# Seven block products for one gate and up projection, and a grouped down projection, in a two-layer backbone block

## The chip, the cores and the metric

The kernel runs on one core of a Trainium2 chip. The metric is the device time of one execution in microseconds (us). Engines are named as the profile names them: PE is TensorE (its matrix products; PEld are its weight loads), DVE is VectorE, ACT is ScalarE, POOL is GpSimd, and SP issues the transfers.

## What is computed

A block of two layers works on 512 latent tokens of 1024 features (plus 256 context tokens in layer 0). Each layer is a mixer and a SwiGLU feed-forward network (FFN) with 2816 hidden features, both behind a modulated RMS norm and a gated residual:

```
mod = silu(c) @ ada_w[i] + ada_b[i]
sh1, sc1, g1, sh2, sc2, g2 = split(mod, 6)
hx = rms_norm(x, norm_mix[i]) * (1 + sc1) + sh1
x = x + g1 * mixer_i(hx)              # layer 0: attention and SSD; layer 1: gated short convolution
h = rms_norm(x, norm_ffn[i]) * (1 + sc2) + sh2
x = x + g2 * ((silu(h @ w_gate) * (h @ w_up)) @ w_down)
...
return rms_norm(x, final_norm)
```

## The kernel before

Activations are kept transposed, features on the 128 partitions and tokens along the columns: xT is 8 tiles (k) of 128 x 512. The 512 tokens are often handled as two halves (e = 0, 1) of 256. A matrix is multiplied in float32r with a split: value = hi + lo, and `mm3` issues three products for each 128 x 128 block, hi x hi, hi x lo and lo x hi.

Weights come in the order of one list, `plan`. `weight` loads 128 x 1024 values into a staging tile (wst, 3 buffers), ScalarE casts them to whi (L94) and VectorE subtracts to get wlo (L95); both have 3 buffers. `take` hands out the next piece and asks for the one two places further. At two seams a fourth buffer from another pool (`extra`) is used, so that three pieces for the next stage and the one behind them can be ready.

After a mixer or an FFN, `project` multiplies by the output weights, adds into xT (L916) and squares for the next norm. Its last tiles (`tail`: 3 after the mixers, 1 after the FFNs) are done in halves of 256 columns, first half 0 of all, then half 1. For each half a job `renorm` is put in the list `due`: after 3500 further columns of products it issues the statistics (L333) and nine tiny VectorE instructions for the inverse root (L142 to L150), after 8500 more the broadcast (L307), and then `entry`, which makes the modulated activation of that half, k by k, and splits it into act_hi and act_lo (L945 to L952). `mm3` counts the columns by `tick`; `flush` issues what is left, and `tick` with a huge count goes on through the whole list.

In `ffn` the first three pieces are multiplied together by `together` (the joint loop), k outermost, first half 0 and then half 1, so that TensorE can follow the entry. Then come 22 hidden tiles f, each gate and up with 24 products of 512 columns, into PSUM (psS); `finish` applies silu and the product and splits into ffn_h. All 22 hidden tiles are kept; only then `project` runs over them with 66 products for each of 8 output tiles. During FFN 0 the generator `ada_rest` computes modulation rows in the background: each step is one load of 256 KB (ada_st) and one VectorE instruction (L257), a product with the constant `fold` ends it, and `pump(3)` lets it advance three steps after each piece.

TensorE's instructions are issued in the order in which the program writes them. The other engines' queues are ordered by a scheduler at build time, by that order and by its own expectation of when operands are ready; on the chip every queue runs in order.

Of the kernel before, what the change touches and what calls it, by code (L numbers as in the profile page):

```python
# [7 lines left out]
F32 = mybir.dt.float32  # L8
# [31 lines left out]
NCON = CAT[-1]  # L40

# [12 lines left out]

def halves(ap):
    return ap.rearrange("p (a b) -> p a b", a=2)


class Block:
    def __init__(self, ctx, tc, t):  # L60
# [3 lines left out]
        self.plan, self.ready, self.used = [], [], 0  # L64
# [6 lines left out]
        self.plan += [(t["w_o"][d], 1024) for d in range(KC)]  # L71
        for i in range(2):
            if i == 1:
                self.plan += [(t["w_sc"][j, x], 1024, j == 0 and x == 1) for j in range(KC) for x in (1, 2, 0)]
                self.plan += [(t["w_so"][d], 1024) for d in range(KC)]
            self.plan += [(t["w_gu"][i, f, x], 1024, f + x == 0) for f in range(NF) for x in range(2)]
            for d in range(KC):
                self.plan += [(t["w_dn"][i, d, :, k:min(k + KC, NF), :], P * min(KC, NF - k)) for k in range(0, NF, KC)]
# [17 lines left out]

    def take(self, ahead=2):
        n = self.used
        self.used += 1
        for i in range(len(self.ready), min(n + ahead + 1, len(self.plan))):  # L100
            self.ready.append(self.weight(*self.plan[i]))
        w, self.ready[n] = self.ready[n], None
        return w

    def weight(self, src, n, extra=False):
# [3 lines left out]
        hi, lo = ((self.np if extra else self.wp).tile([P, 1024], F32R, name=x, tag=x, bufs=1 if extra else 3)  # L109
                  for x in ("whi", "wlo"))  # L110
        self.split(hi[:, :n], lo[:, :n], st[:, :n])
        return hi, lo
# [123 lines left out]
    def ada_rest(self, pool, layer, parts, acc=None, bufs=2, tag=None):  # L236
# [3 lines left out]
        for n, part in enumerate(parts):  # L240
            for j in range(2):
# [4 lines left out]
                for k in range(0, KC, step):  # L246
                    if acc is None:
# [91 lines left out]
    def hybrid(self):  # L339
# [5 lines left out]
        with tc.tile_pool(name="start", bufs=1) as sp:  # L345
# [22 lines left out]
            def weights():  # L368
                for i in range(3):
                    self.ready.append(self.weight(*self.plan[i]))  # L370
# [526 lines left out]
    def project(self, xt, m, gate, between, nk=KC, order=None, tail=1, lead=0, more=True):  # L897
# [32 lines left out]
        ws = [load(2 + more - i) for i in range(tail)]  # L930
# [6 lines left out]
    def entry(self, xt, i, j):  # L937
        nc = self.nc
        gsc, sh = self.gsc[:, i, j, :], self.mod[:, i, 3 * j, :]

        def run(e, rb):
            ts = slice(TC * e, TC * e + TC)
            for k in range(KC):
                u = self.np.tile([P, TC], F32, name="nm_u", tag="nm_u", bufs=3)
                nc.vector.tensor_tensor(u, xt[:, k, ts], rb, ALU.mult)  # L945
                if k % 2:
                    nc.vector.tensor_scalar(u, u, gsc[:, k:k + 1], sh[:, k:k + 1], ALU.mult, ALU.add)
                else:
# [193 lines left out]
```

## Time and profile before

| | |
|---|---|
| median of 3 runs | 1294.58 us (1290.67 to 1295.09) |
| the profiled execution | 1294.68 us, span 1292.9 us |
| mean granted TensorE clock | 0.989 of full speed |
| busy: PE, DVE, ACT, POOL | 1241.5, 731.7, 448.0, 182.7 us |
| FFN 0 | about 370 to 735 us |
| short convolution layer | about 735 to 916 us |
| FFN 1 | about 916 to 1281 us |

The span is from the first to the last instruction of the profiled execution; the time has 1.8 us around it. Products are pipelined, and a product's own duration is longer than the distance to the next one: for TensorE the starts are to be read. The granted clock 1.00 is 2.4 GHz, and 0.50 is 1.2 GHz.

### The profile page before, as it was taken

How to read it: one execution, taken by the hardware profiler on the slowest of the kernel's cores; microseconds unless marked ns; L12 is line 12 of the kernel's file. 1: busy time of each engine (PE TensorE's matmuls, PEld its weight loads, DVE VectorE, ACT ScalarE, POOL GpSimd, SP SyncE). 2: the span in 40 equal slices, each digit the busy share in tenths (PEclk: the TensorE clock that was granted, in tenths of full speed). 3: DMA queues.
4: the chain of work that ended last, by engine and by line, in shares of the span. 5: the costliest groups of instructions: out<-in, count | busy, mean ns of one | idle time of the engine just before them, and what ended most of it. 6: DMA issues, size and time to landing. Idle time of an engine off the chain costs nothing.

```text
span 1292.9 us, 15877 instructions
## 1 busy us (share of the span) xinstructions
PE 1241.5 (96%) x6086; PEld 1022.4 (79%) x6086; DVE 731.7 (57%) x1187; ACT 448.0 (35%) x675; POOL 182.7 (14%) x199
## 2 busy tenths in 40 slices
PE   5999988899999999999999999999999999999997
PEld 3887665567798888888888988888988888888886
DVE  4898899976464777788522564443643333332223
ACT  4534534455353222222222342223532222222221
POOL 3433435440220000000000110002200000000001
PEclk9998989999999999999999999999999999999998
DMA  9331453300413777777433323333133333333322
GB/s 370 125 98 49 123 166 119 98 1 1 149 63 122 229 250 241 226 235 255 123 102 90 115 67 97 98 98 114 50 114 98 98 98 98 92 96 90 92 88 66
DMA packets 54845, 158.52 MB, mean 123 GB/s; under 512 B 6000, under 2 KB 8688, under 8 KB 54512
## 3 DMA queue, kind: packets, MB, share of 16 engines
q1 hardware_dynamic: 54480, 157.20, 38.3%
q8 instruction: 48, 0.79, 0.3%
q10 hardware_dynamic: 288, 0.31, 0.1%
q14 instruction: 29, 0.24, 0.1%
HBM read 154.86 MB, written 2.10 MB: 121 GB/s over the span
## 4 chain that ended last, share of the span: by engine, by line
PE 83%; DVE 9%; issue 3%; DMA 3%; POOL 1%; ACT 1%; SPq 0%; DVEq 0%; ACTq 0%; POOLq 0%
PE psS L116 14%; PE psS L117 14%; PE psS L118 14%; PE psA L116 10%; PE psA L118 10%; PE psA L117 10%; PE psV L830 2%; DMA adaw<-ada 2%; PE psS L961 1%; DVE xtok L257 1%; DVE mx L804 1%; PE psS L822 1%; DVE wlo L95 1%; PE psS L963 1%; DMA xT<-xT 1%
## 5 line engine op out<-in xcount | busy, mean ns | idle before, releaser
L95 DVE TENSOR_TENSOR wlo<-wst,whi 128x1024 fp32r<-128x1024 f32 (+2 forms) x194 | 234.9, 1214 | 317.2 <-ACT whi L94 311.8
L94 ACT CAST whi<-wst 128x1024 fp32r<-128x1024 f32 (+2 forms) x194 | 198.4, 1026 | 549.9 <-PE psS L117 258.5
L116 PE MATMUL psS<-act_hi,whi 128*128 128x512 f32 x760 | 297.5, 391 | 1.0 <-DVE cs_a L573 0.9
L118 PE MATMUL psS<-act_hi,wlo 128*128 128x512 f32 x760 | 297.2, 391 | 0.0
L117 PE MATMUL psS<-act_lo,whi 128*128 128x512 f32 x760 | 297.2, 391 | 0.0
L118 PEld LDWEIGHTS psS<-act_hi,wlo 128*128 128x128 f32 x760 | 143.3, 189 | 30.0
L116 PEld LDWEIGHTS psS<-act_hi,whi 128*128 128x128 f32 x760 | 143.2, 188 | 29.3 <-issue 1.2
L117 PEld LDWEIGHTS psS<-act_lo,whi 128*128 128x128 f32 x760 | 143.2, 188 | 27.7
L325 POOL TENSOR_TENSOR sq_acc<-sq_acc,sq 128x512 f32<-128x512 f32 (+1 forms) x28 | 38.0, 1356 | 872.2 <-issue 645.7
L116 PE MATMUL psA<-ffn_h_hi,whi 128*128 128x512 f32 (+1 forms) x396 | 145.4, 367 | 0.0
L117 PE MATMUL psA<-ffn_h_lo,whi 128*128 128x512 f32 (+1 forms) x396 | 145.0, 366 | 0.0
L118 PE MATMUL psA<-ffn_h_hi,wlo 128*128 128x512 f32 (+1 forms) x396 | 145.0, 366 | 0.0
L257 DVE SCALAR_TENSOR_TENSOR ada_acc<-ada_st,silu_c,ada_acc 128x512 f32<-128x512 f32 x98 | 73.5, 750 | 25.5 <-DMA ada_st<-ada 24.0
L117 PEld LDWEIGHTS psA<-ffn_h_lo,whi 128*128 128x128 f32 x396 | 74.7, 189 | 12.0
L118 PEld LDWEIGHTS psA<-ffn_h_hi,wlo 128*128 128x128 f32 x396 | 74.7, 189 | 12.1
L116 PEld LDWEIGHTS psA<-ffn_h_hi,whi 128*128 128x128 f32 x396 | 74.7, 189 | 11.9
L116 PE MATMUL psA<-act_hi,whi 128*128 128x512 f32 (+1 forms) x216 | 80.0, 370 | 0.1
L118 PE MATMUL psA<-act_hi,wlo 128*128 128x512 f32 (+1 forms) x216 | 79.2, 367 | 0.8 <-DVE wlo L95 0.8
L117 PE MATMUL psA<-act_lo,whi 128*128 128x512 f32 (+1 forms) x216 | 79.6, 368 | 0.0
L916 DVE SCALAR_TENSOR_TENSOR xT<-psA,mod,xT 128x512 f32<-128x512 f32 (+1 forms) x40 | 25.6, 643 | 67.9 <-PE psA L118 67.7
L94 ACT CAST ffn_h_hi<-sg 128x512 fp32r<-128x512 f32 x44 | 27.3, 621 | 59.0 <-DVE sg L980 59.0
L118 PEld LDWEIGHTS psA<-act_hi,wlo 128*128 128x128 f32 x216 | 40.8, 189 | 8.1 <-DVE wlo L95 1.3
(297 smaller groups left out, 1810.7 us busy)
## 6 DMA issues: line engine op xcount, KB each, us to landing
wst<-w_gu SPq DMA_DIRECT2D x88, 512.0 KB, 3.6
ada_st<-ada SPq DMA_DIRECT2D x112, 256.0 KB, 4.0
wst<-w_dn SPq DMA_DIRECT2D x32, 512.0 KB, 3.5
wst<-ada SPq DMA_DIRECT2D x24, 512.0 KB, 3.8
wst<-w_sc SPq DMA_DIRECT2D x24, 512.0 KB, 3.7
adaw<-ada SPq DMA_DIRECT2D x16, 512.0 KB, 10.4
wst<-w_dn SPq DMA_DIRECT2D x16, 384.0 KB, 3.2
wst<-w_f SPq DMA_DIRECT2D x10, 512.0 KB, 3.6
```

The source lines that it names most:

```text
L94: nc.scalar.copy(hi, src)
L95: nc.vector.tensor_tensor(lo, src, hi.bitcast(F32), ALU.subtract)
L116: nc.tensor.matmul(out, lhsT=a[0], rhs=b[0], start=start, stop=False)
L117: nc.tensor.matmul(out, lhsT=a[0], rhs=b[1], start=False, stop=False)
L118: nc.tensor.matmul(out, lhsT=a[1], rhs=b[0], start=False, stop=stop)
L257: nc.vector.scalar_tensor_tensor(a, w[:, i], c, a, ALU.mult, ALU.add)
L325: nc.gpsimd.tensor_tensor(self.acc[:, ts], self.acc[:, ts], sq, ALU.add)
L804: nc.vector.tensor_reduce(mx[:, c:c + 1], s[:, 0:768], AX.X, ALU.max)
L822: nc.tensor.matmul(s[:, a * T:a * T + T], lhsT=kt[x][:, ks], rhs=q[x], start=(x == 0), stop=(x == 1))
L830: nc.tensor.matmul(av, lhsT=vz[:, kc, vs], rhs=e[:, a], start=(c + a == 0), stop=(c + a == CHUNKS - 1))
L916: nc.vector.scalar_tensor_tensor(xt[:, d, ts], ps, gate[:, d:d + 1], xt[:, d, ts], ALU.mult, ALU.add)
L961: nc.tensor.matmul(out, lhsT=a[:, k * P:(k + 1) * P], rhs=hi, start=(k == 0 and a is w[0]), stop=False)
```

## The change

Gate and up of FFN 1 are seen as a 2 x 2 block matrix (gate and up weights by the two halves of the 8 feature tiles) that multiplies a 2 x 2 block activation (the two halves of the features by the two halves of the tokens). Instead of eight block products of 4 tiles and 256 columns, seven are formed, with sums of blocks on both sides. The sums of the activation are made in `combine` when half 1 enters, those of the weights by GpSimd for each hidden tile, and the block products are added up on VectorE. A hidden tile f is three steps: A (2 block products, one weight piece), B (3) and C (2).

In both FFNs the hidden tiles are kept only in groups of 5, 5, 4, 4 and 4: after the tile behind a group, `down` multiplies the group by its part of the output weights and adds into all 8 tiles of xT. The last group goes through `project`, which now has 4 hidden tiles; `lead=3` in FFN 1 starts three output tiles without the last hidden tile.

The list of weights may now hold callables; `feed` prepares pieces as long as fewer than 3 large (of them the one in use) and 5 small ones are held. The fourth buffer at the seams is gone. The modulation rows 3 to 5 of layer 1 move from FFN 0 into the short convolution, with `pump(7)` after each of its 8 tiles; their loads have 2 buffers of their own, and in FFN 0 the advance begins at f = 2 instead of 4.

```diff
+SEVEN = (1,)
+GROUPS = ((0, 5), (5, 10), (10, 14), (14, 18), (18, 22))
+def steps():
+    out = [("A", 0), ("A", 1), ("A", 2), None]
+    for f in range(NF):
+        out += [("A", f)] * (f > 2) + [("B", f), ("C", f)]
+        out += [("D", g) for g in range(len(GROUPS) - 1) if GROUPS[g][1] == f]
+    return out
...
+        def first():
+            st = raw[f] = self.wp.tile([P, 1024], F32, name="wst", tag="wst", bufs=3)
+            nc.sync.dma_start(out=st, in_=t["w_gu"][i, f, 0])
+            return self.rounded(self.wp, "whi", "wlo", 3, st)
+        def sums():
+            a1, a2 = raw[f], self.sv.tile([P, 1024], F32, name="wsu", tag="wsu", bufs=2)
+            nc.sync.dma_start(out=a2, in_=t["w_gu"][i, f, 1])
...
+            nc.gpsimd.tensor_tensor(st[:, h[1]], a2[:, h[0]], a2[:, h[1]], ALU.add)
+            nc.gpsimd.tensor_tensor(st[:, h[0]], st[:, h[1]], a1[:, h[0]], ALU.subtract)
+            nc.gpsimd.tensor_tensor(s3, a1[:, h[0]], a2[:, h[0]], ALU.subtract)
+            nc.gpsimd.tensor_tensor(s4, a1[:, h[1]], st[:, h[0]], ALU.subtract)
+            raw[f] = s3, s4, a2[:, h[1]]
+            return self.rounded(self.wp, "whi", "wlo", 3, st)
+        def small(x):
+            return lambda: self.rounded(self.sv, "qhi", "qlo", QUARTERS, raw[f][x])
+        return {"A": [first], "B": [sums, small(0)], "C": [small(1), small(2)]}[kind]
...
+    def feed(self):
+        while self.made < len(self.plan):
+            x = self.plan[self.made]
+            large = sum(1 for w, n in self.pieces[self.freed:] if n > 512)
+            if large >= 3 or len(self.pieces) - self.freed - large >= QUARTERS:
+                return
+            self.pieces.append(x() if callable(x) else self.weight(*x))
+            self.made += 1
...
-        ws = [load(2 + more - i) for i in range(tail)]
+        ws = [load(2 - i) for i in range(tail)]
...
+        def combine(rb):
+            for k in range(4):
+                u = []
+                for x in (k, k + 4):
+                    u.append(self.np.tile([P, TC], F32, name="nm_u", tag="nm_u", bufs=3))
+                    nc.vector.tensor_tensor(u[-1], xt[:, x, TC:], rb, ALU.mult)
+                    affine(u[-1], x, nc.scalar)
+                t1, t4 = self.u0[:, k], self.u0[:, k + 4]
+                t2 = self.np.tile([P, TC], F32, name="nm_t", tag="nm_t", bufs=2)
+                nc.vector.tensor_tensor(t1, u[0], t1, ALU.subtract)
+                nc.vector.tensor_tensor(t2, u[1], t1, ALU.subtract)
+                split(self.sums(0, k), t2, nc.vector)
+                split(self.act.at(k, 1), t1, nc.vector)
+                nc.gpsimd.tensor_tensor(u[0], u[1], u[0], ALU.subtract)
+                split(self.sums(1, k), u[0], nc.gpsimd)
+                split(self.act.at(k + 4, 1), u[1], nc.vector)
+                nc.gpsimd.tensor_tensor(t4, t4, t2, ALU.subtract)
+                split(self.sums(2, k), t4, nc.gpsimd)
...
+            def down(g):
+                for d in range(KC):
+                    w = self.take()
+                    ps = self.psA()
+                    lo, hi = GROUPS[g]
+                    for k in range(lo, hi):
+                        c = slice((k - lo) * P, (k - lo + 1) * P)
+                        self.mm3(ps, [a[:, c] for a in w], hid.at(k), k == lo, k == hi - 1)
+                    nc.vector.scalar_tensor_tensor(xt[:, d], ps, gate[:, d:d + 1], xt[:, d], ALU.mult, ALU.add)
+                    self.pump(1)
...
-            self.project(xt, hid, self.mod[:, i, 5, :], after, NF, more=(i == 0))
+            self.project(xt, Shifted(hid, lo), gate, after, hi - lo, lead=3 * (i in SEVEN), more=(i == 0))
...
+            if kind == "A":
+                product(ps[:, 0], half(p, 0), b11)
+                nc.scalar.copy(cs[:, 2], ps[:, 0])
+                product(ps[:, 1], half(p, 1), b21)
+                add(cs[:, 0], ps[:, 1], cs[:, 2])
...
+            elif kind == "B":
+                product(ps[:, 0], half(p, 0), t2)
+                add(cs[:, 2], ps[:, 0], cs[:, 2])
+                product(ps[:, 2], q, t3)
+                add(cs[:, 3], ps[:, 2], cs[:, 2])
+                product(ps[:, 1], half(p, 1), t1)
+                z = ps[:, 1]
+                add(cs[:, 1:3], z[:, None].broadcast_to([P, 2, TC]), cs[:, 2:4])
+            else:
+                product(ps[:, 0], p, b22)
+                product(ps[:, 1], q, t4)
+                add(cs[:, 1:4:2], ps, cs[:, 1:4:2])
+                g = cs[:, 0:2]
+                nc.scalar.activation(g, g, AF.Silu)
+                for e in range(2):
+                    nc.vector.tensor_tensor(g[:, e], g[:, e], cs[:, 3 - e], ALU.mult)
+                hi, lo = hid.new(f)
+                nc.scalar.copy(hi, g)
+                nc.gpsimd.tensor_tensor(lo, g, hi.bitcast(F32), ALU.subtract)
```

## Rows read from the trace of the kernel before

**Rows 1.** The page, busy time, share and instructions of each engine.

```profile
PE 1241.5 (96%) x6086; PEld 1022.4 (79%) x6086; DVE 731.7 (57%) x1187; ACT 448.0 (35%) x675; POOL 182.7 (14%) x199
```

**Rows 2.** Windows: stretch, length, busy us (instructions) by engine, PEclk, DMA share, GB/s.

```profile
1000.00:1100.00 100.00, 100.00 (x443) 82.84 (x442) 33.92 (x37) 29.61 (x37) 0.00 (x0) 1.00 0.32 99
```

**Rows 3.** Timeline of TensorE, halves of 256 columns: start, us, instruction.

```profile
897.46 0.28 PE L116 MATMUL psA<-sconv_h_hi,whi 128*128 128x256 f32 x1
...
907.77 0.28 PE L118 MATMUL psA<-sconv_h_hi,wlo 128*128 128x256 f32 x1
```

**Rows 4.** Groups by line and shape: count, busy us, mean ns, idle before.

```profile
L95 DVE TENSOR_TENSOR wlo<-wst,whi 128x1024 fp32r<-128x1024 f32 x174 | 216.5, 1247 | 307.7 <-ACT whi L94 303.1 <-DMA wst<-w_gu 2.9
L257 DVE SCALAR_TENSOR_TENSOR ada_acc<-ada_st,silu_c,ada_acc 128x512 f32<-128x512 f32 x98 | 73.5, 750 | 25.5 <-DMA ada_st<-ada 24.0
L95 DVE TENSOR_TENSOR ffn_h_lo<-sg,ffn_h_hi 128x512 fp32r<-128x512 f32 x44 | 30.2, 686 | 15.8 <-ACT ffn_h_hi L94 15.8
L916 DVE SCALAR_TENSOR_TENSOR xT<-psA,mod,xT 128x512 f32<-128x512 f32 x24 | 17.9, 750 | 43.8 <-PE psA L118 43.8
L951 ACT CAST act_hi<-nm_u 128x256 fp32r<-128x256 f32 x48 | 18.5, 404 | 9.9 <-DVE nm_u L947 9.0
L949 ACT ACTIVATE nm_u<-nm_u,mod,gsc 128x256 f32<-128x256 f32 x24 | 14.4, 602 | 8.7 <-DVE nm_u L945 8.5
L952 DVE TENSOR_TENSOR act_lo<-nm_u,act_hi 128x256 fp32r<-128x256 f32 x24 | 9.9, 418 | 0.4
```

**Rows 5.** Timeline of VectorE: roots at two seams, splits beside GpSimd.

```profile
341.00 3.45 DVE L95 TENSOR_TENSOR wlo<-wst,whi 128x1024 fp32r<-128x1024 f32 x2
...
371.72 1.55 DVE L95 TENSOR_TENSOR wlo<-wst,whi 128x1024 fp32r<-128x1024 f32 x1
...
728.82 0.16 DVE L142 TENSOR_SCALAR rs_v<-psV 128x2 f32<-128x2 f32 x1 [2.10 <-PE psV L333]
...
730.39 0.16 DVE L150 SCALAR_TENSOR_TENSOR rs_y<-rs_t,rs_y 128x2 f32<-128x2 f32 x1
...
736.90 1.22 DVE L95 TENSOR_TENSOR wlo<-wst,whi 128x1024 fp32r<-128x1024 f32 x1
...
740.53 0.16 DVE L142 TENSOR_SCALAR rs_v<-psV 128x2 f32<-128x2 f32 x1 [0.69 <-PE psV L333]
...
743.92 0.59 DVE L150 SCALAR_TENSOR_TENSOR rs_y<-rs_t,rs_y 128x2 f32<-128x2 f32 x1
```

**Rows 6.** Timeline of TensorE at the seams, idle time before in brackets.

```profile
736.71 0.39 PE L961 MATMUL psA<-act_hi,whi 128*128 128x256 f32 x1 [1.04 <-DVE xT L916]
...
739.09 0.50 PE L963 MATMUL psA<-act_lo,whi 128*128 128x256 f32 x2 [0.57 <-POOL act_lo L952]
...
916.33 0.28 PE L961 MATMUL psS<-act_hi,whi 128*128 128x256 f32 x1
...
924.73 0.71 PE L307 MATMUL psA<-cons,rs_y 128*128 128x128 f32 x4 [0.28 <-DVE rs_y L150]
```

**Rows 7.** Timeline of ScalarE at the start of FFN 0.

```profile
370.02 1.05 ACT L94 CAST whi<-wst 128x1024 fp32r<-128x1024 f32 x1 [0.43 <-PE psA L117]
```

**Rows 8.** Windows early in the kernel and at its end.

```profile
30.00:40.00 10.00, 7.52 (x67) 4.83 (x63) 10.00 (x24) 5.27 (x9) 3.57 (x4) 0.83 0.78 303
...
1284.00:1285.00 1.00, 0.00 (x0) 0.00 (x0) 0.83 (x6) 0.00 (x0) 0.00 (x0) 0.50 0.30 99
```

**Rows 9.** The tile of the modulation loads: from issue to landing.

```profile
L251 SPq DMA_DIRECT2D ada_st<-ada x112: 327/328/432, 414.2 to 617.1; - x112
...
DMA to landing us min/median/max: 2.8/4.0/5.6
```

**Rows 10.** Timeline of GpSimd, alone and beside VectorE.

```profile
341.76 3.84 POOL L325 TENSOR_TENSOR sq_acc<-sq_acc,sq 128x512 f32<-128x512 f32 x2 [52.99 <-ACT sq L322]
...
719.94 1.29 POOL L325 TENSOR_TENSOR sq_acc<-sq_acc,sq 128x512 f32<-128x512 f32 x1 [13.67 <-ACT sq L322]
...
737.09 1.95 POOL L952 TENSOR_TENSOR act_lo<-nm_u,act_hi 128x256 fp32r<-128x256 f32 x1 [15.86 <-ACT act_hi L951]
...
923.50 0.76 POOL L952 TENSOR_TENSOR act_lo<-nm_u,act_hi 128x256 fp32r<-128x256 f32 x1 [0.86 <-ACT act_hi L951]
```

More of the change, by code (lines that the diff above doesn't have):

```diff
@@ L80, in pool, with rounded @@
+    def rounded(self, pool, hi, lo, bufs, src):
+        n = src.shape[-1]
+        w = [pool.tile([P, n], F32R, name=x, tag=x, bufs=bufs) for x in (hi, lo)]
+        self.split(*w, src)
+        return w, n
     def pool(self, name, bufs=1, **kw):
@@ L99, in take, with get, release, weight @@
         self.used += 1
[L100 to L105, printed above, removed]
+        self.release(n + ahead - 2)
+        return self.pieces[n][0]
+    def get(self):
+        self.feed()
+        self.used += 1
+        return self.pieces[self.used - 1][0]
+    def release(self, n):
+        for x in range(self.freed, n):
+            self.pieces[x] = None, self.pieces[x][1]
+        self.freed = max(self.freed, n)
+        self.feed()
+    def weight(self, src, n):
         nc = self.nc
@@ L368, in weights @@
             def weights():
-                for i in range(3):
-                    self.ready.append(self.weight(*self.plan[i]))
+                self.feed()
             load(ct, "ctxT")
@@ new lines, in ffn, with gated, up, finish @@
+            (self.gated_seven if i in SEVEN else self.gated)(fp, hid, down)
+            lo, hi = GROUPS[-1]
+            self.project(xt, Shifted(hid, lo), gate, after, hi - lo, lead=3 * (i in SEVEN), more=(i == 0))
+            self.pump(1000)
+    def gated(self, fp, hid, down):
+        nc = self.nc
+        def up(gu, x, w):
+            for k in range(KC):
+                self.mm3(gu[:, x], [a[:, k * P:(k + 1) * P] for a in w], self.act.at(k), k == 0, k == KC - 1)
+        def finish(f, gu):
+            sg = fp.tile([P, T], F32, name="sg", tag="sg", bufs=3)
+            nc.scalar.activation(sg, gu[:, 0], AF.Silu)
+            nc.vector.tensor_tensor(sg, sg, gu[:, 1], ALU.mult)
+            self.split(*hid.new(f), halves(sg))
+        def banks():
+            return self.psS().rearrange("p (a b) -> p a b", a=2)
+        g0, g1 = banks(), banks()
+        first = [(g0, 0, self.take(2)), (g0, 1, self.take(1)), (g1, 0, self.take(0))]
+        self.flush(1)
+        for e in range(2):
+            self.together([(halves(gu[:, x])[:, e], w) for gu, x, w in first], e)
+            self.flush()
+        finish(0, g0)
+        up(g1, 1, self.take())
+        finish(1, g1)
+        for f in range(2, NF):
+            gu = banks()
+            for x in range(2):
+                up(gu, x, self.take())
+                if f > 1:
+                    self.pump(3)
+            finish(f, gu)
+            for g in range(len(GROUPS) - 1):
+                if GROUPS[g][1] == f:
+                    down(g)
```

157 lines of the change are left out of this document (109 added, 48 removed).

## The prediction

> **What bounds the kernel now.** I read the page's busy shares first: TensorE is busy 96% of the span [rows 1]. Then the windows: a 100 us stretch inside the second FFN holds 443 products of 512 columns at the full granted clock, so one costs 0.226 us and TensorE never waits there [rows 2]. The reader is to see that VectorE is busy for only a third of that window: an FFN is priced by its products. In TensorE's timeline I took the spacing of products of 256 columns: from 897.46 to 907.77 us there are 86 steps, 0.120 us each [rows 3]. So half the columns cost 53% of the time. Last I read the seams, where first products wait for a normalised activation.
>
> **What the change removes.** Gate and up of the second FFN are 22 x 2 x 8 x 3 = 1056 products, of which 72 run as 144 halves: 984 x 0.226 + 144 x 0.120 = 239.7 us. After it, 22 tiles x 7 block products x 4 x 3 = 1848 products of 256 columns: 221.8 us. One eighth of the work is dropped, but only 17.9 us of 240. In each FFN the last output tile, which is done in halves, shrinks from 22 hidden tiles to 4: 132 x 0.120 becomes 24 x 0.120 + 54 x 0.226, 0.8 us, twice. **TensorE saves 19.4 us.** The down projection has as many products as before; its 32 further additions into xT per FFN (0.75 us each [rows 4]) lie under the 12 or 15 products, 2.7 to 3.4 us, of the next output tile and cost nothing; uncovered they would be 24 us.
>
> **The seams.** Both FFNs now end in a tail of one tile with 4 hidden tiles: the second half is 24/2 = 12 products, 3072 columns, fewer than the 3500 after which the first half's statistics are due. So the flush at the next stage issues both normalisations back to back in TensorE's order. Before, 16896 columns covered the first. After FFN0: statistics 0 start 1.5 us after the first half's end, the root alone takes 1.7 us (728.82 to 730.55), broadcast 0.6, statistics 1 0.9, the second root among the entry's instructions 4 us (740.53 to 744.51) [rows 5], broadcast 0.6. Together 10.6 us, of which 1.4 are products and 3.0 statistics and broadcasts that were there before: 6.2 us idle in place of 1.6 now (1.04 + 0.57) [rows 6]: +4.5 (3 to 7). At the end of the kernel the same pair is serial and the first half's outputs delay the second root: +3.5 (2 to 6).
>
> The extra fourth weight buffer goes. At the start of FFN0 the third weight can be cast only when the tail's last weight is free: the cast that now begins at 370.02 takes 1.05 [rows 7], the subtraction behind it 1.55 beside GpSimd [rows 5], 1.25 alone [rows 4]; the joint loop needs it 0.6 us after its start at 369.9: +2. Behind each joint loop (FFN0 and short convolution) the next weight has the same wait, 0.6 + 1.05 + 1.25: +3 each. And FFN0's projection meets its newest hidden tile after 9 products instead of 63: +1.
>
> TensorE's clock: when it idled at the end of the kernel the granted clock fell from 1.00 to 0.50, that is 1.2 GHz; the window from 30 to 40 us has 0.83 on average after idle time, so 3.4 us of it at the low level [rows 8], worth 1.7 us. I add 2 at the seam into the short convolution and 2 at that into the second FFN.
>
> **FFN0's modulation rows.** The parts of layer 1 move partly into the short convolution, and their loads get two buffers instead of a share of four. A load lands in 2.8 to 5.6 us, median 4.0 [rows 9]; with 0.75 for the VectorE step [rows 4] and 0.2 for signals, two buffers give a step per 1.9 to 2.5 us, where the loop advances six per hidden tile, one per 1.8 us. The queue that issues them also carries the weights, and the product that folds them stands in TensorE's order at advance 17 and 66. By 2.2 us a step the first fold comes 2 us late, the second 4 (its group phases advance only one per 3.4 us): +6 (0 at 1.9 us a step; 4 + 13 at 2.5). In the short convolution seven steps take 15.8 of 16.3 us: hidden; at 2.5 its 9 us of lag still fit the lead of 10.
>
> **The start of FFN1.** The joint loop lets k be consumed as the entry makes it: it starts at 916.33, and the entry's last k is there at 924.26 [rows 6, 10]. Three first products A replace it, and the first wants all eight k at once: A0 ends at 924.4 instead of 919.2. A1 ends at 927.3, broadcast 928.0. Then the second half's entry also forms three sums and splits them: per k of four, GpSimd four instructions of 256 columns (0.76), VectorE five subtractions with both operands in SBUF (0.42) and two products with PSUM, ScalarE two of 0.60 and five of 0.40 [rows 4, 10]. The two kinds of engine don't run side by side: around 341 us two splits of 1024 (1.23 alone) and two additions of 512 (1.29 alone) together last from 341.00 to 345.60, 4.6 us, though each engine shows only waiting; at 737.09 a GpSimd instruction of 0.76 lasts 1.95 because a split began before it [rows 5, 10]. So a k costs (4 x 0.76 + 5 x 0.42) x 4.6/5.0 = 4.7 us by that exclusion, four 19; the third sum's last part is ready at 945.5, the fourth's at 947, and with three more block products tile 0 ends at 950 instead of 916.3 + 132 x 0.120 + 1.5 = 933.7: **+16** (10, if only GpSimd's own 3.0 us per k counts, to 23, if the next tile's sums of 5 us go first).
>
> **The loop of FFN1.** Per hidden tile GpSimd adds 4 x 512 and splits 512 (5 x 1.29 = 6.45), VectorE has splits of 1024, 1024 and 3 x 512 and two products of 256 in SBUF (2 x 1.23 + 3 x 0.69 + 2 x 0.42 = 5.4). In series 11.8 us; in the proportion of the 341 us rows (4.6 for 5.0) 10.8. TensorE needs 84 x 0.120 = 10.1. So the pair VectorE plus GpSimd is the limit by a little. The buffers hold about 7 us of it ready when a group phase ends, so later stretches of 4 or 5 tiles lose 0 to 2; the first, whose tiles 1 and 2 have only 60 products left (7.2 against 9.6), loses 7. **+8** (0 to 38, the top being 22 x 1.7 with no lead).
>
> The Trainium skill, SBUF — State Buffer, "Who interferes with whom", says that a VectorE instruction with two SBUF inputs and a GpSimd instruction that reads SBUF exclude each other for a whole instruction; the trace agrees (1.95 in place of 0.76). The same page, "A bandwidth-pool intuition that's wrong (but worth ruling out)", puts a hand-over at about 115 ns, where the rows at 341 us leave none; ten hand-overs a tile would make 11.9 us by its figure, an estimate, and the loop's cost some 30 instead of 8.
>
> **Sum**, against the profiled execution's own 1294.7 us (span 1292.9, 1.8 around it; the median of the runs is 1294.6): -19.4; FFN0's start 2 + 3; modulation 6; FFN0's end 1 + 4.5 + 3; clock 4; FFN1's start 16; its loop 8; end 3.5. That is +51 - 19.4 = +31.6: **1326 us**. All low bounds (2 + 0 + 5 + 10 + 0 + 2: FFN0's start, modulation, the seam after it, FFN1's start, its loop, the end) leave the time at 1294, all high ones (6 + 17 + 13 + 25 + 38 + 6) reach 1380.
>
> **Rivals.**
> Not slower: the vector work of FFN1 stays hidden. For it speaks that VectorE is busy only a third of that stage now, and that GpSimd is all but idle there; against it the exclusion. Then 16 + 2 + 8 go: 1300, inside what can be told from no change; it decides once FFN1's own waits total under 1.5 us.
> The exclusion holds with no lead at all: 11.8 us a tile over 22 tiles, 38 instead of 8: 1356. For it: in-order queues in which a split waits behind a sum that waits for GpSimd; against it: the group phases of 22 to 27 us with little vector work. The page named above, with its hand-over, points this way.
> The two load buffers bind FFN0: at the median landing 2.5 us a step, both folds late and weights queued behind them: 17 instead of 6, 1337. Against it: the lower landings of 2.8.
> The hidden start and loop of FFN1, and all other waits at their low bounds too (2 + 5 + 2): 1284.
>
> **Chances.** Forecast 0.55, of it nearly all slower; hidden 0.12; exclusion without lead 0.16; load buffers 0.08; both 0.09. Under 0.5% (6.5 us) this kernel's runs can't tell a change from none. So slower 0.79, same 0.12, faster 0.09. The range 1288 to 1360 leaves out about 0.09 below and 0.1 above.
>
> **What would show it.** Products of 256 columns 0.120 us apart in FFN1; TensorE idle 10 us or more before its first B product, with the releaser a GpSimd or VectorE split; GpSimd instructions of 512 columns above 1.29 us on average; idle time of 6 us with a low clock before the short convolution's first product; the fold of the modulation rows waiting for VectorE. I am wrong if TensorE in FFN1 runs without gaps from the first B on, or if the seams issue the second normalisation later than I read the flush.

## The result, and the profile after

The changed kernel takes **1446.7 us** (median, 1444.8 to 1450.4), against 1294.4 us for the kernel before on the same chip: a ratio of 1.119, 95% interval 1.115 to 1.122. I had forecast 1326 and a range up to 1360. Slower was right; the size, +152 instead of +32, was not.

The head of the page of after, with the busy time and share of each engine and the granted clock in 40 slices:

```profile
span 1446.2 us, 17983 instructions
...
PE 1277.8 (88%) x6700; PEld 1070.9 (74%) x6700; DVE 902.8 (62%) x1475; ACT 507.5 (35%) x811; POOL 350.4 (24%) x321
...
PEclk9999999999799999999996999996899899999998
```

TensorE's busy share fell from 96% [rows 1] to 88%. No engine has become the bound in its place: VectorE is at 62% of a longer span. TensorE waits. For whom, the table of its waits in after says (engine, tile and line that waited, who released it, us in total, times, longest):

```profile
PE psS L219 <- DVE seven L1175: 42.7, 44, 4.2
PE psA L410 <- DVE rs_y L253: 28.2, 6, 12.7
PE psA L219 <- ACT seven L1184: 13.1, 22, 2.0
```

The first and third rows are new and come in multiples of the 22 hidden tiles: 44 is two in each B step of FFN 1, 22 one in each A step. L1175 is the addition `add`, L1184 the copy of A11 B11 to SBUF. Both read a product out of PSUM, and TensorE waits for them *before the next block product*. The second row is the reciprocal root of the normalisations at the seams, 28.2 us instead of 2.4 before.

Where the time lies is seen in the windows of after (us of the window, busy time and instructions of PE, PEld, DVE, ACT, POOL, then granted clock, DMA share, GB/s):

```profile
760.00:790.00 30.00, 12.09 (x68) 11.44 (x67) 23.35 (x58) 10.59 (x23) 7.03 (x6) 0.60 0.47 159
...
980.00:1020.00 40.00, 23.34 (x102) 19.41 (x103) 31.51 (x54) 17.80 (x42) 26.98 (x26) 0.60 0.08 26
1020.00:1100.00 80.00, 69.70 (x479) 64.31 (x479) 49.46 (x67) 27.78 (x41) 26.63 (x19) 0.97 0.25 72
1100.00:1400.00 300.00, 258.98 (x1658) 235.01 (x1657) 170.84 (x242) 103.55 (x153) 107.61 (x78) 0.96 0.26 78
```

These are the seam into the short convolution, the start of FFN 1, and its loop. In the loop TensorE idles 41 of 300 us while VectorE is busy for 171: neither is full. That is what a chain of short waits between engines looks like, and it is the largest loss. In the windows at 760 and at 980 us the clock of 0.60 adds to the idle time.

One tile of that loop, in the timelines of TensorE, VectorE and GpSimd of after (start, duration, engine, line, out<-in, and in brackets the idle time before it with its releaser):

```profile
1213.00 0.39 PE L219 MATMUL psA<-act_hi,whi 128*128 128x256 f32 x1 [0.46 <-ACT seven L1184]
...
1220.33 0.58 PE L219 MATMUL psS<-tsum_hi,qhi 128*128 128x256 f32 x1 [4.19 <-DVE seven L1175]
1220.71 0.41 PE L220 MATMUL psS<-tsum_lo,qhi 128*128 128x256 f32 x1
...
1223.78 0.39 PE L219 MATMUL psS<-act_hi,whi 128*128 128x256 f32 x1 [0.52 <-DVE seven L1175]
```
```profile
1217.77 0.69 DVE L180 TENSOR_TENSOR qlo<-ws,qhi 128x512 fp32r<-128x512 f32 x1 [2.54 <-ACT qhi L179]
1218.71 1.23 DVE L180 TENSOR_TENSOR wlo<-wsa,whi 128x1024 fp32r<-128x1024 f32 x1 [0.26 <-ACT whi L179]
1219.86 0.42 DVE L1175 TENSOR_TENSOR seven<-psS,seven 128x256 f32<-128x256 f32 x1
```
```profile
1212.01 2.36 POOL L147 TENSOR_TENSOR wsa<-wsu 128x512 f32<-128x512 f32 x1
1214.45 1.29 POOL L148 TENSOR_TENSOR wsa<-wsa,wst 128x512 f32<-128x512 f32 x1
1215.82 1.26 POOL L150 TENSOR_TENSOR ws<-wst,wsa 128x512 f32<-128x512 f32 x1
```

A plain stop is 0.46 to 0.52 us: a read of 0.37 (the copy) or 0.42 (the addition), and the signals. At 1220 us it is 4.19. The addition that frees the PSUM tile takes 0.42 us, but it stands in VectorE's queue behind two splits; those wait for casts of sums for the next hidden tile, which GpSimd finishes only at 1217. So the stop on PSUM ties TensorE to the preparation of weights that it doesn't need yet. After the stop its products are 0.21 us apart instead of 0.120 [rows 3]: from 1220.3 to 1223.0 us the granted clock is 0.50, that is 1.2 GHz.

The second finding is at the start of FFN 0, in VectorE's timeline of after:

```profile
364.74 0.16 DVE L245 TENSOR_SCALAR rs_v<-psV 128x2 f32<-128x2 f32 x1 [0.70 <-PE psV L436]
365.08 0.76 DVE L360 SCALAR_TENSOR_TENSOR u_first<-ada_st,silu_c,u_first 128x512 f32<-128x512 f32 x1 [0.19 <-DMA ada_st<-ada]
365.75 0.16 DVE L246 TENSOR_SCALAR rs_y<-rs_v 128x2 int32<-128x2 int32 x1
...
374.20 0.16 DVE L253 SCALAR_TENSOR_TENSOR rs_y<-rs_t,rs_y 128x2 f32<-128x2 f32 x1
```

Nine root instructions of about 0.16 us take 9.6 us (to 374.36), since steps of the modulation (L360) that wait for their loads, and other work, stand between them. The same root took 4.0 us before, from 362.48 to 366.46:

```profile
362.48 0.16 DVE L142 TENSOR_SCALAR rs_v<-psV 128x2 f32<-128x2 f32 x1 [2.10 <-PE psV L333]
...
365.76 0.70 DVE L150 SCALAR_TENSOR_TENSOR rs_y<-rs_t,rs_y 128x2 f32<-128x2 f32 x1
```

These steps were not there before the change, as the rows of that tile show, before and after (instruction, duration min/median/max in ns, first and last start):

```profile
L255 DVE TENSOR_SCALAR ada_acc<-ada_st,silu_c x14: 475/477/480, 419.8 to 611.0; 128x512 f32<-128x512 f32 x14
```
```profile
L358 DVE TENSOR_SCALAR u_first<-ada_st,silu_c x14: 476/483/1509, 342.3 to 855.1; 128x512 f32<-128x512 f32 x14
```

### The profile page after: what moved, and what is told of

Same layout as the page of the kernel before. It is cut to its first block, busy times and chain, and to the rows that moved or that the text cites. A ratio compares the mean times of both kernels' runs of the same rounds, so it can differ in the third digit from the quotient of the medians.

```text
span 1446.2 us, 17983 instructions
## 1 busy us (share of the span) xinstructions
PE 1277.8 (88%) x6700; PEld 1070.9 (74%) x6700; DVE 902.8 (62%) x1475; ACT 507.5 (35%) x811; POOL 350.4 (24%) x321
## 4 chain that ended last, share of the span: by engine, by line
PE 60%; DVE 16%; DMA 13%; issue 5%; POOL 3%; ACT 3%; SPq 0%; DVEq 0%; POOLq 0%; ACTq 0%
PE psA L219 9%; PE psA L220 9%; PE psA L221 9%; PE psS L219 9%; PE psS L221 8%; PE psS L220 8%; DMA ada_st<-ada 8%; DVE u_first L360 2%; DVE wlo L180 2%; PE psV L932 2%; DMA adaw<-ada 1%; DVE seven L1175 1%; DMA wst<-w_gu 1%; ACT whi L179 1%; DVE xtok L360 1%
## 5 line engine op out<-in xcount | busy, mean ns | idle before, releaser
L179 ACT CAST whi<-wst 128x1024 fp32r<-128x1024 f32 (+3 forms) x204 | 181.4, 892 | 440.7 <-PE psS L220 211.9
L180 DVE TENSOR_TENSOR wlo<-wst,whi 128x1024 fp32r<-128x1024 f32 (+3 forms) x204 | 218.7, 1074 | 137.7 <-ACT whi L179 135.2
L219 PE MATMUL psS<-act_hi,whi 128*128 128x512 f32 (+1 forms) x520 | 199.0, 383 | 22.5 <-DVE seven L1175 17.3
L221 PE MATMUL psS<-act_hi,wlo 128*128 128x512 f32 (+1 forms) x520 | 196.5, 378 | 2.3 <-DVE wlo L180 2.3
L220 PE MATMUL psS<-act_lo,whi 128*128 128x512 f32 (+1 forms) x520 | 195.8, 377 | 0.0
L219 PE MATMUL psA<-act_hi,whi 128*128 128x256 f32 (+1 forms) x392 | 137.4, 351 | 14.5 <-ACT seven L1184 13.1
L221 PE MATMUL psA<-act_hi,wlo 128*128 128x256 f32 (+1 forms) x392 | 134.0, 342 | 5.8 <-DVE wlo L180 5.8
L220 PE MATMUL psA<-act_lo,whi 128*128 128x256 f32 (+1 forms) x392 | 134.6, 343 | 2.4 <-DVE act_lo L1052 2.0
L360 DVE SCALAR_TENSOR_TENSOR u_first<-ada_st,silu_c,u_first 128x512 f32<-128x512 f32 x98 | 77.1, 787 | 58.8 <-DMA ada_st<-ada 58.1
L220 PEld LDWEIGHTS psS<-act_lo,whi 128*128 128x128 f32 x520 | 100.2, 193 | 15.5
L219 PEld LDWEIGHTS psA<-act_hi,whi 128*128 128x128 f32 x392 | 79.2, 202 | 26.6 <-ACT seven L1184 17.6
L220 PEld LDWEIGHTS psA<-act_lo,whi 128*128 128x128 f32 x392 | 79.1, 202 | 10.8 <-DVE act_lo L1052 2.8
```

The costliest lines, as they stand in the source:

```text
L179: nc.scalar.copy(hi, src)
L180: nc.vector.tensor_tensor(lo, src, hi.bitcast(F32), ALU.subtract)
L219: nc.tensor.matmul(out, lhsT=a[0], rhs=b[0], start=start, stop=False)
L220: nc.tensor.matmul(out, lhsT=a[0], rhs=b[1], start=False, stop=False)
L221: nc.tensor.matmul(out, lhsT=a[1], rhs=b[0], start=False, stop=stop)
L360: nc.vector.scalar_tensor_tensor(a, w[:, i], c, a, ALU.mult, ALU.add)
```

## The experiments

Each is compared with runs of the kernel before on the same chip, where that kernel took 1293.3 to 1294.2 us. The medians are of all executions; the table also cuts the span of the one profiled execution of each kernel into three stages: up to the last product of FFN 0's joint loop; from there to the last product of the short convolution's projection; and FFN 1 to the end. The borders are the last starts of the groups of products of the joint loop (wlo) and on the tile sconv_h_hi (wlo), here for before and after; the number ahead of the semicolon is the border:

```profile
L961 PE MATMUL psS<-act_hi,wlo x48: 279/284/284, 370.1 to 389.2; 128*128 128x256 f32 x48
...
L118 PE MATMUL psA<-sconv_h_hi,wlo x88: 278/284/390, 870.7 to 916.2; 128*128 128x256 f32 x48, 128*128 128x512 f32 x40
```
```profile
L1094 PE MATMUL psS<-act_hi,wlo x48: 279/283/513, 380.6 to 409.2; 128*128 128x256 f32 x48
...
L221 PE MATMUL psA<-sconv_h_hi,wlo x88: 279/389/415, 929.5 to 978.1; 128*128 128x256 f32 x48, 128*128 128x512 f32 x40
```

| kernel | median, us | ratio to before (95%) | stage 1 | stage 2 | stage 3 |
|---|---|---|---|---|---|
| before | 1294.4 | 1 | 389.2 | 527.0 | 376.7 |
| after | 1446.7 | 1.119 (1.115 to 1.122) | 409.2 | 568.9 | 468.1 |
| e1 PSUM tiles | 1378.9 | 1.067 (1.065 to 1.069) | 409.3 | 566.7 | 400.6 |
| e2 loads back | 1407.6 | 1.088 (1.086 to 1.091) | 388.9 | 545.3 | 471.6 |
| e3 eight products | 1370.6 | 1.059 (1.057 to 1.062) | 419.8 | 564.0 | 385.6 |
| e4 eight, loads back | 1319.6 | 1.020 (1.018 to 1.023) | 388.1 | 541.6 | 384.0 |
| e5 = e1 + e2 | 1339.0 | 1.036 (1.033 to 1.038) | 387.2 | 544.8 | 402.8 |
| e6 = e5, entry on VectorE | 1335.2 | 1.032 (1.030 to 1.035) | 389.3 | 543.3 | 398.5 |
| e7 = e5, sums on VectorE | 1322.3 | 1.023 (1.020 to 1.025) | 386.0 | 543.7 | 389.1 |
| e8 = e5, flush | 1333.1 | 1.032 (1.029 to 1.035) | 387.0 | 541.5 | 401.0 |
| e9 = e5 to e8 | 1321.9 | 1.021 (1.020 to 1.023) | 390.4 | 539.2 | 387.3 |
| e10 = e9, two plain tiles | 1312.4 | 1.013 (1.011 to 1.015) | 390.0 | 544.7 | 378.8 |
| e11 = e9, tails of three | 1319.0 | 1.019 (1.018 to 1.021) | 388.9 | 540.9 | 385.5 |
| e12 eight, grouped, mended | 1314.8 | 1.016 (1.012 to 1.019) | 389.2 | 541.8 | 386.3 |
| e13 = e10, FFN 0 as before | 1301.9 | 1.006 (1.004 to 1.008) | 385.8 | 531.9 | 378.1 |
| e14 = e13, fourth buffer | 1295.2 | 1.001 (1.000 to 1.002) | 387.2 | 526.9 | 378.3 |
| e15 = e14, FFN 1's ends | 1290.6 | 0.997 (0.996 to 0.998) | 389.4 | 527.1 | 373.2 |

**First four runs: the two large causes.** Theory 1: the PSUM stops and the early modulation loads hold most of the loss. The rival is that the clock, or the seven products' vector work as forecast, does.

```diff
 e1 (after, A step; B likewise)
-ps = self.psA((P, 2, TC))
-product(ps[:, 0], half(p, 0), b11)
-product(ps[:, 1], half(p, 1), b21)
+ps, ps1 = self.psA((P, TC)), self.psA((P, TC))
+product(ps, half(p, 0), b11)
+product(ps1, half(p, 1), b21)
```

The two products of step C, which one addition reads together, keep one tile.

> The five block products of a hidden tile that share a PSUM tile with another get tiles of their own; all else as in the changed kernel (1446.7). Theory 1: TensorE stops 66 times in FFN 1 until an addition or a copy has read the product before it in the same PSUM tile (56 us of waits in the changed kernel, 51 of them for VectorE's additions or ScalarE's copy from the second tile on), so the time falls by 40 to 60 us, to 1387 to 1407. Theory 2: the shared access of VectorE and GpSimd limits the loop at 10.8 to 11.8 us a tile, the stops only show where the lateness surfaces, and it will surface as waits for weight splits: less than 20 us are gained, 1427 or more.

```diff
 e2 (after): modulation loads in the shared sg buffers, all in FFN 0
-yield from self.ada_rest(fp, 0, (5,), acc, bufs=2, tag="ada_st")
-yield from self.ada_rest(fp, 1, range(3), acc, bufs=2, tag="ada_st")
+yield from self.ada_rest(fp, 0, (5,), acc, bufs=4, tag="sg")
+yield from self.ada_rest(fp, 1, range(6), acc, bufs=4, tag="sg")
```

The silu tile sg has four buffers again, and the three parts in the short convolution go.

> The modulation loads take their place in FFN 0 again (six parts, tiles from the four buffers of the silu tile, none in the short convolution); seven products and groups stay. Theory 1: buffers of their own let the scheduler put the modulation steps ahead of the roots at both seams, and VectorE waits there for their loads: FFN 0's start (21 us later than before), the seam after FFN 0 (22) and part of the short convolution's 8 come back except for the 5, 8 and 3 that I priced for the seams themselves, 35 us: about 1411. Theory 2: the seams are late because of the short tail and the missing fourth weight buffer: less than 12 us, 1435 or more.

e3 sets `SEVEN = ()`, so that gate and up of FFN 1 are eight products again and only grouping with its short tails, loads and buffers differ from before; e4 does this and e2's edit.

> FFN 1 with eight block products as in FFN 0 (no sums, no A, B, C steps), the rest of the change as it is. FFN 1 with the end takes 470 us in the changed kernel against 377 before. Theory 1: nearly all of these 93 us belong to the seven products: 1446.7 - 93 + 18 (the products saved) would count twice, so 1357 to 1365 with the seam costs that stay. Theory 2: grouping the down projection costs FFN 1 some 20 us by itself: 1375 or more.

> Eight products and the modulation loads as before: only the grouped down projection, the short tail and the list without a fourth buffer stay. Theory 1: the seams cost what I priced, 2 + 3 + 1 + 4.5 + 3 + 2 + 3.5 = 19 us, less 1.5: 1312. Rival: the grouped projection with its 32 further additions per FFN is hidden and the seams too: 1295 to 1300.

e1 took off 67.8 us, more than the 40 to 60 of theory 1; 67.5 of them lie in stage 3. Windows over that stage, in after and in e1:

```profile
978.10:1446.20 468.10, 385.56 (x2426) 347.68 (x2425) 275.07 (x417) 167.34 (x267) 174.71 (x134) 0.92 0.24 71
```
```profile
976.00:1376.60 400.60, 362.13 (x2427) 335.39 (x2425) 296.83 (x417) 160.54 (x267) 185.24 (x134) 0.94 0.28 83
```

For the same products TensorE is idle for 38.5 us instead of 82.5, and busy for 23.4 us less, at a higher mean clock. In e1's windows of the loop the clock is at 1.00, and TensorE is busy for 235 of 240 us:

```profile
1100.00:1340.00 240.00, 235.03 (x1654) 220.45 (x1653) 183.25 (x236) 94.06 (x147) 109.86 (x73) 1.00 0.31 91
```

So what made TensorE wait was that two block products shared a PSUM tile, and nothing that the products themselves need. (Whether the chip needs that wait, or the program only places it because both products name one tile, no run separates. Nine waits, 8.2 us in all, for an addition that has yet to free a psA tile are left in e1.) e2 took off 39.1 us: 20.3 in stage 1 and 23.6 in stage 2, with 3.5 given back in stage 3; its first step on ada_st is at 402.4 us, and the waits for the root fall from 28.2 to 11.4 us. It takes back buffers of their own, their number and the parts in the short convolution at once; what each of these cost isn't shown. e3 (1370.6) came out between theory 1 and its rival: without the seven products the early loads cost 51 us (e3 to e4), 12 more than with them. e4 was 8 over its forecast. What it keeps (grouping, short tails, no fourth weight buffer) costs 26 us.

**Second four: do the causes add, and what is the third?** All stand on e5. e6 replaces `nc.gpsimd` by `nc.vector` in `combine` (two differences and two splits for each k), e7 in the four instructions of `sums`, and e8 is this:

```diff
 while len(self.due) > n:
-    self.tick(1 << 30)
+    for _ in self.due.pop(0)[0]:
+        pass
```

> A PSUM tile for each block product and the modulation loads back in the old shared buffers, together. Theory 1 (the stops on half-read PSUM tiles lie in the second FFN, the early loads cost time in the first FFN and at its seams, two places that don't touch): the two savings add, 1446.7 - 67.8 - 39.1 = 1340 us, give or take 5. Rival (the two share a part of the time, for instance the clock at the seam ahead of the second FFN): 1350 or more.

> As the run before it, and in the entry to the second FFN GpSimd's four instructions for each k (a difference, the two splits' subtractions, another difference) go to VectorE. Theory 1 (VectorE and GpSimd exclude each other, GpSimd's 0.90 stands in series with VectorE's 0.94 us for two SBUF operands): four instructions of 0.76 to 0.90 become four of 0.42, 4 x 4 x 0.4 = 6 us off the start, 1330 to 1336 us. Rival (the engines work beside each other and VectorE alone is late): VectorE gets 16 x 0.42 = 6.7 us more, 1345 or more.

> As the first run, and the four sums of weights of each hidden tile of the second FFN go from GpSimd to VectorE. Theory 1 (exclusion: a sum on GpSimd takes VectorE's time too): no slower, 1332 to 1343 us, since 4 x 1.29 us of the shared time become 4 x 0.69 and the tile's series falls from 11.8 to 9.4 us, under TensorE's 10.1. Rival (independent engines): VectorE's own work rises by 2.8 us a tile over TensorE's 10.1 us, 1355 or more.

> As the first run, but where a stage begins only the first half's normalisation is issued at once, the second half's stays due after its count of columns. Theory 1 (the two roots back to back at the seams into the short convolution and at the start of the second FFN are part of their stops, and the clock falls in them): 5 to 15 us off, 1325 to 1335 us, nearly all of it between 760 and 800 us. Rival (the second half's statistics are late by themselves, the order doesn't matter): within 3 us of the first run.

e5 is 1339.0: the two savings add. In e7 VectorE has more to do, 88 additions and subtractions of 512 columns that GpSimd had before, and the kernel is 16.7 us *faster* (13.7 of it in stage 3), more than theory 1 asked. That GpSimd was merely the slower engine for them, and nothing was shared, is a rival that the windows over stage 3 settle, e5 and then e7:

```profile
932.00:1334.80 402.80, 362.66 (x2427) 335.59 (x2425) 299.62 (x417) 161.01 (x268) 183.97 (x134) 0.94 0.28 83
```
```profile
929.70:1318.80 389.10, 359.34 (x2427) 334.72 (x2425) 301.46 (x499) 165.24 (x267) 64.74 (x52) 0.94 0.29 86
```

VectorE issues 82 instructions more (some records are missing), about 0.69 us each, and is busy for only 1.8 us more. So its other instructions got shorter by some 55 us, an estimate from these numbers. Its splits of 512 columns show it, in the windows from 1000 to 1300 us of e5 and e7 (count, then busy us and mean ns):

```profile
L180 DVE TENSOR_TENSOR qlo<-ws,qhi 128x512 fp32r<-128x512 f32 x35 | 40.1, 1146 | 5.2 <-ACT qhi L179 4.9
```
```profile
L180 DVE TENSOR_TENSOR qlo<-ws,qhi 128x512 fp32r<-128x512 f32 x34 | 24.7, 732 | 0.0
```

GpSimd's groups in e5's loop are longer too; alone such an instruction takes 1.29 us [rows 10]:

```profile
L150 POOL TENSOR_TENSOR ws<-wst,wsa 128x512 f32<-128x512 f32 x12 | 20.6, 1715 | 0.8
```

e6 is worth 3.7 us (4.3 in stage 3), at the low end of theory 1, and again more work on VectorE made it no later. e8 is worth 5.9 us, also at the low end. 3.3 of them lie in stage 2, where the edit acts; 1.8 lie in stage 3, where TensorE's order is the same as in e5, and aren't shown to come from it.

**Third four: what is left.** e9 is e5 with the three edits. e10 lets the first two hidden tiles of FFN 1 run by eight block products, written with the operands that seven products have anyway (the second half of gate is A11 B11 + A11 T1 + A12 B22, T1 being the difference B12 - B11). They need only the first of the four differences, so the other sums are formed while they run:

```diff
-out = [("A", 0), ("A", 1), ("A", 2), None]
-for f in range(NF):
-    out += [("A", f)] * (f > 2) + [("B", f), ("C", f)]
+out = [("E", 0), ("E", 1), ("E", 2), None, ("L", 0), ("L", 2), ("E", 3), ("L", 3)]
+for f in range(2, NF):
+    out += [("A", f), ("B", f), ("C", f)]
...
E: the first half, three pieces of weights together, k outermost
+    self.mm3(p[:, k // 4], [a[:, k * P:(k + 1) * P] for a in w[f]], self.act.at(k, 0), k % 4 == 0, k % 4 == 3)
L: the second half, x = k // 2 + 4 * (k % 2), added to A11 B11
+    self.mm3(p, [a[:, x * P:(x + 1) * P] for a in w[f]], self.act.at(x, 1), k == 0, k == KC - 1)
```

e11 gives the FFNs' last projection `tail=3`, and e12 is the grouped down projection with eight products, loads back, e8's flush and tail of three.

> All five edits together: a PSUM tile for each block product, the modulation loads back, the second FFN's entry and its sums of weights on VectorE, and the flush that issues the surplus normalisation alone. Theory 1 (five separate losses): the savings add, 1339.0 - 3.7 - 16.7 - 5.9 = 1312.7 us, give or take 4. Rival (the edits share time, VectorE now carries all of them): 1320 or more.

> As the run before it, and the first two of the 22 hidden tiles of the second FFN by eight block products, that need only the first difference and the last block of the second half; the other three sums are formed while these products run. 2 x 12 products more (2.9 us). Theory 1 (between 920 and 980 us some 25 us are lost because seven products want all sums before they begin): 14 to 18 us off the run before it, about 1297 us. Rival (the wait is the second normalisation itself and VectorE's work, wherever it is put): under 6 us off, 1307 or more.

> As the first of these runs, and both FFNs' last projections end with three output tiles in halves instead of one, so that 36 products of the second half lie between the two normalisations instead of 12. Theory 1 (the short tail of 12 products leaves the first root uncovered at the first FFN's end and at the kernel's end): 5 to 10 us off, 1303 to 1308 us. Rival (three weights to be freed at once delay the next stage's first weights as much): within 2 us.

> The grouped down projection alone (gate and up by eight products in both FFNs), with the modulation loads back, the flush that issues one normalisation, and the tail of three. Theory 1 (what grouping costs is its seams): of the 26 us that the same without flush and tail is over the kernel before, 10 to 15 go: 1305 to 1310 us; the fourth weight buffer's waits stay. Rival (grouping costs in its own products): 1316 or more.

e9 missed: 1321.9 instead of 1312.7, the rival's side. By stages, stage 2 adds up (-1.5 - 1.1 - 3.3 = -5.9 forecast, -5.6 measured), stage 3 does not (-4.3 - 13.7 - 1.8 = -19.8 forecast, -15.5 measured): both moves to VectorE work on the same start of FFN 1 and may share 4 us of it, which no run separates. The rest is stage 1, whose code the three edits hardly touch: it came out 3.2 us longer than in e5.

e10 is 9.6 us faster than e9, between its theory and its rival. Its own stage shows the mechanism, in windows of TensorE over FFN 1's start (busy, clock, DMA share, GB/s), e9 and then e10:

```profile
940.00:960.00 20.00, 11.79 (x64) 0.67 0.18 53
960.00:980.00 20.00, 16.48 (x112) 0.78 0.13 33
```
```profile
940.00:960.00 20.00, 15.77 (x95) 0.76 0.18 53
960.00:980.00 20.00, 19.21 (x152) 0.96 0.20 58
```

Stage 3 fell by 8.5 us, although two tiles have one block product more; in the profiled executions 5.5 us are lost again in stage 2, which e10 doesn't edit. The choice of executions is as much: e10's profiled one is the longest of its four (1315.3, median 1312.4), e9's the shortest of its four (1319.2, median 1321.9). e11's tail of three is worth 3 us (1.8 in stage 3, nothing in stage 2): the rival fits FFN 0's end. e12 missed by 5 us: a grouped FFN 0 and FFN 1 with eight products stay at 1314.8.

**Last three: give FFN 0 back.** e13 keeps all 22 hidden tiles of FFN 0 and projects once at its end, which there is room for as long as the buffers of FFN 1's sums are opened only behind it. It also gives the short convolution its second set of working tiles back, of which the change had left one. e14 adds the fourth weight buffer at the starts of FFN 0 and of the short convolution, as before the change. e15 uses that buffer at FFN 1's start too (`QUARTERS` 3 instead of 5) and ends FFN 1 with `tail=3`.

```diff
-hid = Hidden(fp)
+hid = Hidden(fp) if i in SEVEN else Pair(fp, "ffn_h", NF)
...
+sv = self.mid = es.enter_context(tc.tile_pool(name="mid", bufs=1))   # behind FFN 0
...
-if large >= 3 or len(self.pieces) - self.freed - large >= QUARTERS:
+if large >= 3 + extra or len(self.pieces) - self.freed - large >= QUARTERS:
```

> As the run with the first two tiles by eight products, and the first FFN again as before the change (all 22 hidden tiles kept, one projection at its end), with the sums' buffers opened only behind it. The fourth weight buffer stays away. Stages of the run that it starts from: 369.0 us to the first FFN's first product, 565.5 to the last product of the short convolution's projection, 378.8 from there; of the kernel before 369.9, 546.3, 376.7. Theory 1 (the 19 us of the middle stage come from grouping the first FFN and the missing weight buffer): 550 to 555 us in the middle stage, 1300 to 1306 in all. Rival (they come from the modulation loads or the second FFN's buffers, which stay): 560 or more, 1309 or more.

> As the run before it, and the fourth weight buffer back at the starts of the first FFN and of the short convolution. Theory 1: the middle stage as before the change, 546 to 549 us, so 369 + 547 + 379 + 1.8 = 1297 us in all, 1292 to 1302, not to be told from the kernel before. Rival (the fourth buffer was worth nothing): as the run before it, within 2 us.

> As the run before it (first FFN and short convolution as before the change), the second FFN's first weight also in the fourth buffer (three instead of five buffers for the 512-wide sums pay for it), and its last projection with three output tiles in halves. Theory 1 (what is left in the second FFN is its start, where a third weight's split is 2.4 us late, and its end, where the two normalisations stand 12 products apart): 3 us off each, 378 becomes 372 to 374 us from the short convolution's end, 1288 to 1291 us in all, under the kernel before. Rival (fewer buffers for the sums make the loop wait, or the end is set by the last normalisation whatever the order): 1294 or more.

(Here the middle stage is counted from the joint loop's first product; in the table, from its last. Counted as in the expectations, e13 has 552.9 us there and e14 546.0.) All three came out as theory 1 said, e15 within its interval. e14 can't be told from the kernel before (1.0009, 0.9995 to 1.0023). e15 is the one version under it, by 0.3% (0.9957 to 0.9984); it gains 5.1 us in stage 3 over e14, where 3 + 3 were forecast.

## Why the prediction was wrong, step by step

**What bounds the kernel** was right. The kernel is priced by products, and whatever stops TensorE is paid in full, plus the clock.

**TensorE saves 19.4** can't be read alone. Its count fits (6700 products instead of 6086 [rows 1]: 614 more, where its terms give 612), and so does its 0.120 us a product at the full clock. With two plain tiles (+2.9) and most waits gone, e15's FFN 1 takes 3.5 us less than before; how much of the rest its start and end take isn't separated.

**The loop of FFN 1, +8** is the step that failed. It priced the vector work that seven products need against TensorE's 10.1 us a tile, as if the two ran freely beside each other with some 7 us of lead. It did not ask what TensorE does between two block products of a tile, and its 5.4 us of VectorE work has none of the five additions a tile that read PSUM (0.42 to 0.69 us each). Nothing in the rows of before showed a product into one part of a PSUM tile while another part is read. So it needed a bound of its own: 66 reads (three for each of the 22 tiles) at about 0.5 us are 33 us, and more wherever the read is queued behind something late. The runs showed 67.8 us (e1). The priced part itself was of the right order: taking the sums from GpSimd gave 13.7 us in stage 3 (e7), against 8 forecast. VectorE and GpSimd do exclude each other. They do it at FFN 1's start too, in the timelines of after, GpSimd and then VectorE:

```profile
1014.23 0.90 POOL L1078 TENSOR_TENSOR nm_u<-nm_u 128x256 f32<-128x256 f32 x1
1015.10 0.90 POOL L1081 TENSOR_TENSOR u_first<-u_first,nm_t 128x256 f32<-128x256 f32 x1
```
```profile
1014.47 0.94 DVE L1052 TENSOR_TENSOR act_lo<-u_first,act_hi 128x256 fp32r<-128x256 f32 x1
1015.34 0.94 DVE L1052 TENSOR_TENSOR act_lo<-nm_u,act_hi 128x256 fp32r<-128x256 f32 x1
```

Each engine gets one instruction through per 0.87 us, one of theirs after one of the other's; alone they take 0.76 and 0.42 [rows 4, 10]. The Trainium skill, SBUF — State Buffer, "Who interferes with whom", says that a VectorE instruction with two SBUF inputs and a GpSimd instruction that reads SBUF shut each other out for a whole instruction. The strict alternation agrees; but a pair takes 0.87 us, less than 0.76 + 0.42, so not all of the time that the profile gives an instruction is excluded. The Trainium skill, SBUF — State Buffer, "A bandwidth-pool intuition that's wrong (but worth ruling out)", has about 115 ns from VectorE's end until a transfer goes on whose descriptors GpSimd writes. No such gap shows between these instructions.

**FFN 0's modulation rows, +6 (0 to 17)** was the second step that failed. It counted how fast two buffers can be turned over inside FFN 0, and assumed that their loads start where the program starts them. In the code, a load with buffers of its own waits for no work of FFN 0; at 342 us its first step ran already, and later ones stood in VectorE's queue among the root instructions that gate FFN 0's start. With the shared buffers the first step ran at 419.8 us (before) and 402.4 us (e2). Together with the three parts in the short convolution, whose steps stand among the roots of the seam ahead of it, this cost 39.1 us (e2): 20.3 up to the end of the joint loop, 23.6 between there and FFN 1, and 3.5 came back in FFN 1.

**The start of FFN 1, +16, and the clock** was right in kind and about half the size. Hidden tile 0 was to take 33.7 us from the first product (916.3 to 950) instead of 17.4. In after its products run from the first of these rows to the second, where tile 1's next products begin:

```profile
978.17 0.28 PE L219 MATMUL psA<-act_hi,whi 128*128 128x256 f32 x1
...
1026.40 0.28 PE L219 MATMUL psS<-tsum_hi,whi 128*128 128x256 f32 x1
```

That is 48.2 us, +31. Without the stops on PSUM it is 46.4 us (e1), and without GpSimd's part in the sums still 43.3 us (e9), so the exclusion, by which the term was priced, holds little of it. In e9 the windows of 940 to 980 us still hold 28 us of busy time at clocks of 0.67 and 0.78. e10's two plain tiles took 8.5 us from the stage net, and e15's weight buffer and tail together another 5.1.

**The seams.** The back-to-back normalisations at FFN 0's end (+4.5) were worth 3.3 us in that stage (e8). Those at the kernel's end (+3.5) e8 leaves as they are; there the tail of three gave 1.8 us (e11). The fourth buffer's 2 + 3 + 3 were worth 6.7 us in e14. Up to the last product of the short convolution's joint loop stage 2 got 2.6 us shorter by it, and behind it 2.4, near the 3 each of the forecast; the 2 at FFN 0's start aren't seen (stage 1 is 388.9 us in e2, without the buffer, and 389.2 before). What else the grouped FFN 0 costs is 7.3 us of stage 2 (e9 to e13, 539.2 to 531.9), against a forecast of 1 for meeting its newest tile early, the 12 or 15 products of each group's output tile being taken as free. All of it lies ahead of the end of that joint loop: from there to the end of stage 2 e9 and e13 both take 163.5 us, so the short convolution's second set of working tiles isn't the cause. Which part of the grouping it is wasn't separated.

**The rivals.** None of them held the cause. The exclusion without lead (1356) comes nearest, but its price was that of two engines in series, not of TensorE stopped by their reads. That slower came true is partly luck: 107 of the 152 us are the stops on PSUM and the early loads (67.8 and 39.1), and the sum has neither as it happened.

## What to carry to other kernels

When a change cuts one long accumulation into short ones that are each read out, ask for each product whether it writes into a tile that another engine still has to read, and count the reads: a PSUM tile for each product that is read by itself was worth 68 us here. When a stream of loads gets buffers of its own, look for what held it back until then; its steps can turn up in the queue of an engine that a seam is waiting for. An eighth fewer products (18 us of 1294) paid only after these two, with the sums on VectorE, the stages ahead left as before and the start covered by two plain tiles, and then 0.3% was left.

## What the runs showed of the hardware that was not expected

- An idle time of 4.19 us in a loop was paid twice: behind it 256-column products are 0.21 us apart instead of 0.120, at a granted clock of 0.50. In e1 stage 3 got 44 us shorter by TensorE's idle time and 23 by the shorter busy time of the same products, at a mean clock of 0.94 instead of 0.92.
- Moving 512-column additions with both operands in SBUF from GpSimd to VectorE made the busier engine's kernel faster (16.7 us for 88 of them). VectorE's busy time in stage 3 rose by only 1.8 us, since its own splits no longer last 1.15 us but 0.73.
- Stage 1 of the kernels whose edits hardly touch it (e2 and e4 to e12) ended between 386.0 and 390.4 us, and four executions of one kernel (e10) took 1308.5 to 1315.3. A stage is read from one execution, so 3 us between the stages of two kernels are no more than this spread.
